# Operand places, the routing's place count and a fourth buffer in a mixture-of-experts block

## The chip, the cores and the metric

One core of one Trainium2 chip runs the whole program. The metric is device time in microseconds (us). The kernel before took 1858.37 us, the median of 3 runs (1856.73 to 1860.6). The engines are TensorE (PE, with its weight loads listed as PEld), VectorE (DVE), ScalarE (ACT), GpSimd (POOL) and SyncE (SP, which issues most of the loads).

## The reference, cut to what matters

One transformer block on 1024 tokens of width 1024: a mixer (an mLSTM half and a dilated-attention half, then `w_out`), and an expert-choice feed-forward layer with 16 experts. All is float32. The part that matters here:

```python
def expert_choice_ffn(h, w_router, b_router, w_gate, w_up, w_down):
    cap = (EC_CAPACITY_FACTOR * S) // N_EXPERTS            # 128 tokens an expert
    affinity = jax.nn.softmax((h @ w_router + b_router), axis=-1)
    gates, idx = lax.top_k(affinity.transpose(0, 2, 1), cap)
    xin = h[bidx, idx]
    hid = jax.nn.silu(xin @ w_gate) * (xin @ w_up)         # 1024 -> 2048, each expert
    y = (hid @ w_down) * gates[..., None]                  # 2048 -> 1024
    return jnp.zeros_like(h).at[bidx, idx].add(y)
```

Each expert's three matrices are 8 MB each in float32, so 384 MB of weights are read once.

## The kernel before, in words

**Split products.** Each float32 product is made of three float32r products: an operand x is split into a high part (ACT copies it to float32r) and a low part (DVE subtracts the high part from x), and xh·wh, xl·wh and xh·wl are summed in PSUM. In a product of 128 by 512 one operand is stationary (its 128 columns are loaded by PEld) and the other moves (512 columns). Each product loads its weights anew.

**Pieces.** A weight matrix of an expert comes in 8 pieces of 128 x 2048 float32 (1 MB). `feed` (L1452) issues the load of the next piece on SP, or on a queue that it is given. `cut` (L1479) takes the oldest loaded piece, makes `wh` on ACT (L1489) and `wl` on DVE (L1490, kept in program order on DVE), and issues the next load into the buffer just freed. `mm` (L1495) runs the 12 products of one piece (L1509) and then calls `cut` once. `wh` and `wl` have CUTS = 3 buffers each, so that the piece being cut during the products of piece n is n + 2. Loaded pieces wait in a ring: RING = 10 buffers (6 of them opened before the router's last steps, EARLY), and 3 more pieces made of borrowed tiles.

**Order of the experts** (`phase_experts`, L1570). For expert e: 8 gate pieces, 8 up pieces, then the 8 down pieces of expert e - 1. Between them stand the transposes of the hidden rows (`expert_hT`, L1538), of the next expert's rows (`expert_xT`, L1525, rows fetched by an indirect load, L1443) and the products that turn a one-hot matrix into row numbers (`route_expert`, L1429). The stationary operands are `xTh` (pool moe1), `xTl` (pool y, tag og) and `hT` (pool ya); the moving ones are `wh` and `wl` (pool moe2).

**Places.** A pool is a stack of tiles on the left or right side of each partition. From the sizes of the pools in their order, `wh`, `wl` and `xTh` begin at a multiple of 512 bytes, `xTl` and `hT` 64 bytes past one. In the projections (L337 to L341, L398 to L400) both operands lie 448 bytes past one. In the output projection (L1174 to L1176) the moving parts lie 192 bytes past one, the stationary ones too, but for three of the four `yal` (64).

**Routing** (`route_sort`, `route_select`). The threshold of each expert is the smallest of its 128 best affinities, found by sorts on DVE in streams that the output projection carries along; the last tile of tokens has its sort in `route_select`. Each sort also keeps the transposed affinities (`keep`, L1308). `route_select` compares them with the threshold (L1398, L1399), counts places by a scan along the row (L1401), adds the counts of the segments before (L1405 to L1411), transposes back (L1414) and makes the first one-hot matrix (L1425).

**What orders the work.** The tile framework's planner orders each engine's queue by its own estimate of when work is ready; an engine then runs its queue strictly in order. `keep_in_program_order` holds an instruction behind the one traced before it on its engine.

Of the kernel before, what the change touches and what calls it, by code (L numbers as in the profile page):

```python
# [11 lines left out]
F32 = mybir.dt.float32  # L12
# [8 lines left out]
P = 128  # L21
# [22 lines left out]

RING = 10
EARLY = 6
FEEDS = (2, 8, 14, 20, 26, 32)
LATE = 3
CUTS = 3
HT = (1, 3, 5, 7)  # L50
# [24 lines left out]
def shape_constants():  # L75

    u = np.arange(F1LEN) - 191
    v1 = np.abs(u) <= 64
    da = np.arange(F2ROW) - 63
    db = np.arange(7) - 3  # L80
    r4 = (4 * da[None, :] + db[:, None]).reshape(-1)
    v4 = np.abs(r4) <= 64
    r16 = np.where(np.abs(da) <= 64, da, 0)
    oh = np.concatenate([_onehot(u, v1), _onehot(4 * r4, v4), _onehot(16 * r16, np.ones(F2ROW, bool))], axis=1)
    mask = np.where(np.concatenate([v1, v4, np.ones(F2ROW, bool)]), 0.0, NEG).astype(np.float32)
    turn = np.concatenate([np.arange(F1LEN)[::-1], F1LEN + np.arange(F2LEN + F2ROW).reshape(-1, F2ROW)[:, ::-1].reshape(-1)])
    oh, mask = oh[:, turn], mask[turn]
    seg, ex = np.divmod(np.arange(P), 32)
    same = ex[:, None] == ex[None, :]
    seg_c = np.stack([same & (seg[:, None] < seg[None, :]), same & (seg[:, None] > seg[None, :])], axis=1).astype(np.float32)  # L90
    return {"c_seg": np.ascontiguousarray(seg_c), "c_oh": np.ascontiguousarray(oh), "c_mask": np.ascontiguousarray(np.broadcast_to(mask, (AH, mask.size)))}

# [17 lines left out]
class K:  # L110
# [3 lines left out]
    def pool(self, name, stack, bufs=1, space=None, side=None):  # L114
# [965 lines left out]
    def route_consts(self, ps):  # L1080
# [7 lines left out]
        self.sort_mem = rt.tile([P, KT, P], F32, name="sort_mem")  # L1088
        self.affT = self.sort_mem[:, 6:8]
        self.r_work, self.bit_a, self.bit_b = (itertools.cycle([self.sort_mem[:, j], self.sort_mem[:, j + 1]]) for j in (0, 2, 4))  # L1090
# [194 lines left out]
    def route_sort(self, i0, n, last=False):  # L1285
# [4 lines left out]
        R = 32 * n  # L1290
        self.copy = nc.vector.tensor_copy if last else lambda o, i: nc.scalar.activation(o, i, AF.Copy)
        mx = rt.tile([P, 4], F32, name="r_mx", bufs=2)[:, :n]
# [13 lines left out]
        nc.tensor.transpose(ps[:R, :P], self.aff[:, i0:i0 + n].rearrange("p s e -> p (s e)"), self.ident)  # L1306

        def keep():  # L1308

            i = i0  # L1310
            while i < i0 + n:
                j = min(i0 + n, i + min((4, 1, 2, 1)[i % 4], (4, 1, 2, 1)[i - i0]))
                self.copy(self.affT[32 * (i % 4):32 * (i % 4 + j - i), i // 4], ps[32 * (i - i0):32 * (j - i0), :P])
                i = j

        w = next(self.r_work).rearrange("p (h t) -> p h t", h=2)
        a, b = next(self.bit_a), next(self.bit_b)
        if n > 2:
# [7 lines left out]
            for r in range(8):  # L1326
                for h in range(2):
                    nc.vector.max(top[h][:, 8 * r:8 * r + 8], src[:, h])
                if r < 7:
                    for h in range(2):  # L1330
                        nc.vector.match_replace(w[:, h], top[h][:, 8 * r:8 * r + 8], src[:, h], -1.0)
                    src = w
                if r == 0:
                    keep()
                yield 0
            nc.vector.tensor_copy(a[:R, 64:], t[:R, ::-1])
        else:
# [3 lines left out]
            for h in range(2):  # L1341
                self.copy(x[h * R:(h + 1) * R], ps[:R, 64 * h:64 * h + 64])
            yield 0
            for r in range(8):
                nc.vector.max(a[R2, 8 * r:8 * r + 8], x)
                if r < 7:
                    nc.vector.match_replace(w, a[R2, 8 * r:8 * r + 8], x, -1.0)
                    x = w
                if r == 0:
                    keep()  # L1350
                yield 0
# [33 lines left out]
    def route_select(self):  # L1385


        nc, rt = self.nc, self.rt
        m = self.yp.tile([P, 8, P], F32, name="sel", tag="og", bufs=MH)
        seg = m[:, 4:6]  # L1390
        nc.scalar.dma_start(out=seg, in_=self.I["c_seg"])
# [4 lines left out]
        for r in range(32, P, 32):  # L1396
            nc.vector.tensor_copy(thr[r:r + 32], thr[:32])
        nc.vector.tensor_scalar(m[:, 0:2], self.affT, thr, None, op0=OP.is_gt)  # L1398
        nc.vector.tensor_scalar(m[:, 2:4], self.affT, thr, None, op0=OP.is_equal)  # L1399
        sc = self.yp.tile([P, 4, P], F32, name="r_scan", tag="og", bufs=MH)  # L1400
        nc.vector.tensor_tensor_scan(sc.rearrange("p j t -> p (j t)"), self.ones[:, 0:1].to_broadcast([P, 4 * P]), m[:, 0:4].rearrange("p j t -> p (j t)"),  # L1401
                                     0.0, OP.mult, OP.add)

        ps = self.psm.tile([P, 512], F32, name="pm")
        nc.tensor.matmul(ps[:, :4], seg[:, 0], sc[:, :, P - 1], start=True, stop=False)  # L1405
        nc.tensor.matmul(ps[:, 1:4], seg[:, 1], sc[:, 0:3, P - 1], start=False, stop=True)
        base = rt.tile([P, 4], F32, name="r_base")
        nc.vector.tensor_copy(base, ps[:, :4])
        for j in range(4):
            nc.vector.scalar_tensor_tensor(sc[:, j], sc[:, j], base[:, j:j + 1], m[:, j], op0=OP.add, op1=OP.mult)  # L1410
        nc.vector.tensor_add(sc[:, 0:2], sc[:, 0:2], sc[:, 2:4])  # L1411
        ps = self.psm.tile([P, 4, P], F32, name="pm")
        for g in range(2):
            nc.tensor.transpose(ps[:, g], sc[:, g], self.ident)  # L1414
        self.route_gates()
        sl = ps[:, 0:2].rearrange("p g (s e) -> p (g s) e", e=32)
        self.onehot(0, sl)
        self.slot = rt.tile([P, NT, 32], F32, name="slot")
        nc.vector.tensor_copy(self.slot, sl)

# [7 lines left out]
    def route_expert(self, e, psum):  # L1428
# [6 lines left out]
        for i in range(NT):  # L1435
            nc.tensor.matmul(ps[:, :5], oh[:, i], self.R[:, i, e], start=(i == 0), stop=(i == NT - 1))
        idx = rt.tile([P, 1], I32, name="idx", bufs=3)
        rg = rt.tile([P, 5], F32, name="rg", bufs=3)
# [5 lines left out]
                                     in_offset=bass.IndirectOffsetOnAxis(ap=idx[:, :1], axis=0))  # L1444
        return dict(idx=idx, gate=rg[:, 0:1], xin=xin)

# [31 lines left out]

    def cut(self):  # L1479

        if not self.fed:
            return
        ts, again = self.fed.pop(0)
        h = self.m2.tile([P, FF], F32R, name="wh", bufs=CUTS)
        l = self.m2.tile([P, FF], F32R, name="wl", bufs=CUTS)
        m = FF // len(ts)
        for j, t in enumerate(ts):
            c = slice(j * m, (j + 1) * m)
            self.nc.scalar.activation(h[:, c], t, AF.Copy)  # L1489
            self.tc.keep_in_program_order(self.nc.vector.tensor_sub(l[:, c], t, h[:, c]))  # L1490
        self.ready.append((h, l))
        if again:
            self.feed(ts)

    def mm(self, xs, n, first, last):  # L1495
# [6 lines left out]
        order = [(q, t, c) for q in range(3) for t in range(FF // N) for c in range(len(ps))]  # L1502
        if last and not (self.fed or self.ready):

# [9 lines left out]

    def expert_xT(self, u, b, psum):

# [7 lines left out]
        for k in range(4 * b, 4 * b + 4):  # L1524
            nc.scalar.activation(f[:, k], ps[:, (k % 4) * P:(k % 4 + 1) * P], AF.Identity, scale=self.a2_col[:, k:k + 1], bias=self.modc[:, KT + k:KT + k + 1])  # L1525
        self.split(h[:, 4 * b:4 * b + 4], l[:, 4 * b:4 * b + 4], f[:, 4 * b:4 * b + 4])
# [38 lines left out]
    def phase_experts(self):  # L1565
# [23 lines left out]
        for b in range(2):  # L1589
            self.expert_xT(u, b, sets[1])  # L1590
        self.ahead = 1
        self.cut()
        p = None
        for e in range(NE):
# [29 lines left out]
def body(tc, I, out):  # L1624
    with ExitStack() as ctx:
# [51 lines left out]
        k.ring = [k.pool("ring_a", st_w, bufs=EARLY)]  # L1677
        k.flow, k.fed, k.ready = k.pieces(), [], []
        k.phase_out()
# [43 lines left out]
```

## Time and profile before

| | us |
|---|---|
| median of 3 runs | 1858.37 |
| the profiled execution | 1857.18 |
| its span | 1855.5 |
| PE busy | 1738.8 |
| DVE busy | 1486.8 |
| ACT busy | 1206.2 |
| first to last expert product (starts, L1509) | 682.8 to 1843 |

Busy time is the sum of an engine's instructions; PE's is modelled and overlaps, so the distance between the starts of two products, and not their length, tells how fast they follow each other. A window is a stretch of the span in us from its start.

### The profile page before, as it was taken

The page shows a single profiled execution, that of the slowest core. Times are in us where ns is not written, and L with a number is a line of the kernel's source. Part 1 is how long each engine was busy: PE and PEld are TensorE (multiplying, and loading weights), DVE is VectorE, ACT ScalarE, POOL GpSimd, SP SyncE. Part 2 cuts the span into 40 slices and gives each one's busy share as a digit, 9 for nine tenths or more (in the row PEclk, how much of TensorE's full clock was granted, in tenths as well). Part 3 has the DMA queues.
Part 4 walks back from the last instruction along what each step waited for, and adds up shares of the span by engine and source line. Part 5 has one row for each costly group of instructions (what it writes and reads, how often), then busy time and mean ns, then how long its engine had stood idle before and what let it go on. Part 6 is the DMA issues. An engine that isn't in the chain of part 4 may idle for free. (4 is left out here: it accounts for less than half of the span.)

```text
span 1855.5 us, 24345 instructions
## 1 busy us (share of the span) xinstructions
PE 1738.8 (94%) x8685; PEld 1400.1 (75%) x8685; DVE 1486.8 (80%) x2147; ACT 1206.2 (65%) x1596; POOL 179.6 (10%) x176
## 2 busy tenths in 40 slices
PE   5999999999998939999999999999999999999997
PEld 4777788778886727888888777787777777777875
DVE  5578885687865778988988888898888888988976
ACT  5346454477763438777777677777776776777764
POOL 1001000031122010011011000100100001000001
PEclk9999999999999959999999999999999999999999
DMA  8135662435648777999999999999999999999991
GB/s 321 47 108 188 208 209 89 108 89 118 139 112 239 270 306 278 382 356 371 392 351 389 348 347 351 362 367 358 352 343 383 349 354 360 336 377 356 357 357 23
DMA packets 150536, 517.39 MB, mean 279 GB/s; under 512 B 32938, under 2 KB 50736, under 8 KB 112784
## 3 DMA queue, kind: packets, MB, share of 16 engines
q1 hardware_dynamic: 136832, 482.07, 70.6%
q0 software_dynamic: 10528, 33.18, 7.1%
q8 instruction: 68, 1.11, 0.2%
q10 hardware_dynamic: 3056, 0.61, 0.2%
q14 instruction: 52, 0.43, 0.1%
HBM read 488.29 MB, written 27.50 MB: 278 GB/s over the span
## 5 line engine op out<-in xcount | busy, mean ns | idle before, releaser
L1490 DVE TENSOR_TENSOR wl<-w,wh 128x2048 fp32r<-128x2048 f32 x295 | 663.2, 2279 | 72.9 <-ACT wh L1489 72.0
L1489 ACT ACTIVATE wh<-w 128x2048 fp32r<-128x2048 f32 x295 | 557.7, 1914 | 120.2 <-PE px L1509 56.3
L1490 DVE TENSOR_TENSOR wl<-w_half,wh 128x1024 fp32r<-128x1024 f32 x178 | 207.9, 1218 | 8.3 <-ACT wh L1489 8.2
L1489 ACT ACTIVATE wh<-w_half 128x1024 fp32r<-128x1024 f32 x178 | 179.8, 1059 | 36.8 <-PE px L1509 16.3
L1509 PE MATMUL px<-wl,xTh 128*128 128x512 f32 x512 | 142.5, 398 | 10.0 <-DVE wl L1490 10.0
L1509 PE MATMUL py<-wl,xTh 128*128 128x512 f32 x512 | 142.6, 398 | 8.9 <-DVE wl L1490 8.8
L1509 PE MATMUL px<-wh,xTh 128*128 128x512 f32 x512 | 141.9, 397 | 3.5 <-ACT wh L1489 1.9
L1509 PE MATMUL py<-wh,xTh 128*128 128x512 f32 x512 | 142.6, 396 | 0.8 <-ACT wh L1489 0.7
L1509 PE MATMUL px<-wh,xTl 128*128 128x512 f32 x512 | 141.4, 397 | 0.0
L1509 PE MATMUL py<-wh,xTl 128*128 128x512 f32 x512 | 141.1, 395 | 0.0
L1509 PE MATMUL px<-wh,hT 128*128 128x512 f32 x512 | 131.5, 397 | 0.0
L1509 PE MATMUL py<-wh,hT 128*128 128x512 f32 x512 | 130.8, 397 | 0.2 <-ACT wh L1489 0.2
L1509 PEld LDWEIGHTS px<-wl,xTh 128*128 128x128 f32 x512 | 94.8, 189 | 38.7 <-DVE wl L1490 18.1
L1509 PEld LDWEIGHTS py<-wl,xTh 128*128 128x128 f32 x512 | 94.1, 188 | 38.1 <-DVE wl L1490 17.8
L1562 POOL DMA_INDIRECT out_dram<-xin,idx x16 | 52.6, 3288 | 661.2 <-DVE xin L1561 661.2
L1509 PEld LDWEIGHTS px<-wh,xTh 128*128 128x128 f32 x512 | 95.2, 189 | 26.6 <-ACT wh L1489 3.6
L1509 PEld LDWEIGHTS px<-wh,xTl 128*128 128x128 f32 x512 | 96.8, 189 | 21.9
L1509 PEld LDWEIGHTS py<-wh,hT 128*128 128x128 f32 x512 | 95.1, 188 | 23.4 <-ACT wh L1489 0.9
L1509 PEld LDWEIGHTS py<-wh,xTh 128*128 128x128 f32 x512 | 94.4, 188 | 24.2 <-ACT wh L1489 3.1
L1509 PEld LDWEIGHTS py<-wh,xTl 128*128 128x128 f32 x512 | 96.1, 188 | 21.8 <-DVE xTl L124 0.2
L1509 PEld LDWEIGHTS px<-wh,hT 128*128 128x128 f32 x512 | 95.0, 188 | 22.6 <-ACT wh L1489 0.4
L398 PE MATMUL pa<-wh,hTh 128*128 128x512 f32 x192 | 78.9, 412 | 1.6 <-ACT wh L355 1.5
(452 smaller groups left out, 3091.9 us busy)
## 6 DMA issues: line engine op xcount, KB each, us to landing
w<-in_w_gate_dram SPq DMA_DIRECT2D x99, 1024.0 KB, 7.3
w<-in_w_down_dram SPq DMA_DIRECT2D x99, 1024.0 KB, 9.6
w<-in_w_up_dram SPq DMA_DIRECT2D x94, 1024.0 KB, 6.2
w_half<-in_w_up_dram SPq DMA_DIRECT2D x62, 512.0 KB, 7.2
w_half<-in_w_gate_dram SPq DMA_DIRECT2D x56, 512.0 KB, 8.2
w_half<-in_w_down_dram SPq DMA_DIRECT2D x56, 512.0 KB, 8.7
ada_w<-in_w_ada_dram SPq DMA_DIRECT2D x64, 256.0 KB, 3.4
wraw<-in_w_in_dram SPq DMA_DIRECT2D x20, 512.0 KB, 4.5
```

Of the source, the lines that this page charges most:

```text
L398: nc.tensor.matmul(ps, hTh[:, k, t], hi[k], start=(k == 0), stop=False)
L1489: self.nc.scalar.activation(h[:, c], t, AF.Copy)
L1490: self.tc.keep_in_program_order(self.nc.vector.tensor_sub(l[:, c], t, h[:, c]))
L1509: nc.tensor.matmul(ps[c], x[:, t], y[:, o:o + 512], start=first and q == 0 and t == 0, stop=last and (q, t) == (2, FF // N - 1))
L1562: nc.gpsimd.indirect_dma_start(out=self.out, out_offset=bass.IndirectOffsetOnAxis(ap=u["idx"][:, :1], axis=0), in_=y, in_offset=None, comp ...
```

## The change: what it does

It adds two unused tiles: 448 bytes ahead of pool `consts` (the first on the left) and 192 bytes ahead of the other tiles of pool `rows` (right). All later tiles of these sides move by as much, so that the expert stage's five operands and those of the output projection all begin at a multiple of 512 bytes. It makes RING 8 and CUTS 4, splits `cut` into a high part (`cut_high`) and the rest, and has ACT make three `wh` during the last sort. It leaves out `keep`, the segments' constant and the scan, and counts the places by 16 bfloat16 products with a triangle and a matrix of ones (built on POOL in `route_consts`). It issues the row fetch of the next expert two pieces later than its one-hot products, and in the first expert lets DVE do every second of the eight scalings in `expert_xT`.

```diff
-RING = 10
+RING = 8
-CUTS = 3
+CUTS = 4
...
+    def fill(self, pool, n):
+        self.nc.gpsimd.memset(pool.tile([P, n // 4], F32, name="fill"), 0.0)
...
     def consts(self):
+        self.fill(cp, 448)
...
-                if r == 0:
-                    keep()
...
             for h in range(2):
-                self.copy(x[h * R:(h + 1) * R], ps[:R, 64 * h:64 * h + 64])
+                if last and h == 0:
+                    nc.vector.tensor_copy(x[h * R:(h + 1) * R], ps[:R, 64 * h:64 * h + 64])
+                else:
+                    nc.scalar.activation(x[h * R:(h + 1) * R], ps[:R, 64 * h:64 * h + 64], AF.Copy)
...
     def route_select(self):
-        for _ in self.route_sort(NT - 1, 1, True):
+        sort = self.route_sort(NT - 1, 1, True)
+        next(sort)
+        next(sort)
+        for _ in range(CUTS - 1):
+            self.cut_high()
+        for _ in sort:
             pass
         thr = rt.tile([P, 1], F32, name="thr")
         nc.vector.tensor_reduce(thr[:32], self.best[:32], axis=AX.X, op=OP.min)
-        # thr to all rows, L1398 to L1414: comparison, scan, segments, transposes
...
+        nc.vector.tensor_copy(row[:32], thr[:32].to_broadcast([32, P]))
+        nc.tensor.transpose(ps[:, :32], row[:32], self.ident[:32, :32])
+        nc.vector.tensor_tensor(m[:, 0], aff, t, OP.is_gt)
+        nc.vector.tensor_tensor(m[:, 1], aff, t, OP.is_equal)
+        nc.tensor.matmul(c, self.upto, m, start=True, stop=False)
+        for i in range(NT):
+            nc.tensor.matmul(c[:, 1], self.all_ones, m[:, 0, i:i + 1, :].to_broadcast([P, NT, NE]), start=False, stop=False)
+        for i in range(1, NT):
+            nc.tensor.matmul(c[:, :, i:], self.all_ones, m[:, :, :NT - i], start=False, stop=(i == NT - 1))
         self.route_gates()
+        nc.vector.tensor_mul(f, c, m)
+        nc.vector.tensor_add(self.slot, f[:, 0], f[:, 1])
+        self.onehot(0, self.slot)
...
-    def cut(self):
+    def cut_high(self):
         if not self.fed:
             return
         ts, again = self.fed.pop(0)
         h = self.m2.tile([P, FF], F32R, name="wh", bufs=CUTS)
+        for j, t in enumerate(ts):
+            act = self.nc.scalar.activation(h[:, j * m:(j + 1) * m], t, AF.Copy)
+            if not self.started:
+                self.tc.keep_in_program_order(act)
+        self.halves.append((ts, h, again))
+
+    def cut(self):
+        if not self.halves:
+            self.cut_high()
+        if not self.halves:
+            return
+        ts, h, again = self.halves.pop(0)
         l = self.m2.tile([P, FF], F32R, name="wl", bufs=CUTS)
...
         if again:
-            self.feed(ts)
+            self.feed(ts, None if self.started else self.nc.gpsimd)
...
             if both and k % 2:
+                nc.vector.tensor_scalar(f[:, k], x, g, z, op0=OP.mult, op1=OP.add)
...
-        u = self.route_expert(0, sets[1])
+        _, u = self.route_expert(0, sets[1])
...
                 if e + 1 < NE and i == 0:
-                    n = self.route_expert(e + 1, X)
+                    route = self.route_expert(e + 1, X)
+                    next(route)
+                if e + 1 < NE and i == 2:
+                    n = next(route)
...
         k.rp = k.pool("rows", st_r, side="right")
+        k.fill(k.rp, 192)
```

## Rows read from the trace of the kernel before

**Rows 1.** The page: PE's busy tenths in 40 slices of the span.

```profile
PE   5999999999998939999999999999999999999997
```

**Rows 2.** Windows: length, then busy time (instructions) by engine, granted clock, DMA share, GB/s.

```profile
core 0: us, PE busy (x) PEld busy (x) DVE busy (x) ACT busy (x) POOL busy (x), PEclk, DMA share, GB/s
...
655.00:665.40 10.40, 0.00 (x0) 0.00 (x0) 9.98 (x71) 0.82 (x1) 0.00 (x0) 0.50 1.00 416
...
812.00:882.00 70.00, 70.00 (x322) 56.93 (x321) 62.02 (x47) 53.99 (x49) 7.49 (x3) 1.00 0.97 374
...
1330.00:1405.00 75.00, 72.21 (x325) 56.91 (x324) 62.39 (x46) 52.49 (x48) 5.91 (x2) 1.00 0.97 360
```

**Rows 3.** Timeline of POOL: start, length; one scatter of rows an expert.

```profile
806.41 5.62 POOL L1562 DMA_INDIRECT out_dram<-xin,idx  x1 [42.29 <-DVE xin L1561]
...
1016.45 3.38 POOL L1562 DMA_INDIRECT out_dram<-xin,idx  x1 [40.81 <-DVE xin L1561]
...
1753.09 1.59 POOL L1562 DMA_INDIRECT out_dram<-xin,idx  x1 [42.07 <-DVE xin L1561]
```

**Rows 4.** Waits from 1040 to 1800 us: total, times, longest.

```profile
DVE wl L1490 <- ACT wh L1489: 65.8, 40, 5.8
...
ACT sort_mem L1525 <- PE py L1523: 22.6, 5, 5.0
...
SPq L1472 <- DVE wl L1490: 427.3, 196, 5.9
```

**Rows 5.** Timeline of all engines from 1044 to 1050 us.

```profile
1046.73 0.17 DVE L1439 COPY rg<-py 128x5 f32<-128x5 f32 x1 [0.79 <-PE py L1436]
...
1049.55 1.20 PE L1509 MATMUL px<-wl,xTh 128*128 128x512 f32 x4 [1.36 <-DVE wl L1490]
```

**Rows 6.** Timeline of PE, products of 512 columns in four stages.

```profile
78.79 0.62 PE L337 MATMUL pa<-hTh,wh 128*128 128x512 f32 x2
...
88.31 0.39 PE L337 MATMUL pb<-hTh,wh 128*128 128x512 f32 x1
...
617.20 0.39 PE L1174 MATMUL pm<-woh,mix 128*128 128x512 f32 x1
...
617.88 0.39 PE L1174 MATMUL pm<-woh,mix 128*128 128x512 f32 x1
...
618.57 0.39 PE L1174 MATMUL pm<-wmh,mix 128*128 128x512 f32 x1
...
714.69 1.09 PE L1509 MATMUL py<-wl,xTh 128*128 128x512 f32 x4
...
725.78 1.09 PE L1509 MATMUL py<-wl,xTh 128*128 128x512 f32 x4
...
1006.23 2.03 PE L1509 MATMUL px<-wh,hT 128*128 128x512 f32 x8
...
1009.03 1.33 PE L1509 MATMUL px<-wh,hT 128*128 128x512 f32 x5
```

**Rows 7.** Timeline of all engines from the last affinities to the first expert product.

```profile
653.62 0.37 PE L1306 MATMUL pm<-ident,aff 128*32 128x128 f32 x1 [7.93 <-DVE aff L1304]
...
655.98 0.28 DVE L1313 COPY sort_mem<-pm 32x128 f32<-32x128 f32 x1
...
665.36 0.27 DVE L1395 TENSOR_REDUCE thr<-sort_mem 32x1 f32<-32x128 f32 x1
...
672.29 1.22 DVE L1425 TENSOR_TENSOR oh<-iota,pm 128x1024 bf16<-128x1024 f32 x1 [0.78 <-PE pm L1414]
...
674.85 4.49 DVE L1490 TENSOR_TENSOR wl<-w,wh 128x2048 fp32r<-128x2048 f32 x2 [0.32 <-issue]
...
682.06 0.65 ACT L123 ACTIVATE xTh<-sort_mem 128x512 fp32r<-128x512 f32 x1
...
682.75 2.08 PE L1509 MATMUL px<-wh,xTh 128*128 128x512 f32 x4 [1.61 <-ACT xTh L123]
684.63 1.91 PE L1509 MATMUL px<-wh,xTl 128*128 128x512 f32 x4
```

More of the change, by code (lines that the diff above doesn't have):

```diff
@@ L87, in shape_constants @@
     oh, mask = oh[:, turn], mask[turn]
[L88 to L91, printed above, removed]
+    return {"c_oh": np.ascontiguousarray(oh), "c_mask": np.ascontiguousarray(np.broadcast_to(mask, (AH, mask.size)))}
 def bc(ap, n, offset=0):
@@ L1088, in route_consts @@
         self.sort_mem = rt.tile([P, KT, P], F32, name="sort_mem")
-        self.affT = self.sort_mem[:, 6:8]
+        tri = self.sort_mem[:, 6]
+        nc.gpsimd.memset(tri, 1.0)
+        self.all_ones = rt.tile([P, P], BF16, name="all_ones")
+        nc.gpsimd.tensor_copy(self.all_ones, tri)
+        nc.gpsimd.affine_select(out=tri, in_=tri, compare_op=OP.is_ge, fill=0.0, base=0, pattern=[[1, P]], channel_multiplier=-1)
+        self.upto = rt.tile([P, P], BF16, name="upto")
+        nc.gpsimd.tensor_copy(self.upto, tri)
         self.r_work, self.bit_a, self.bit_b = (itertools.cycle([self.sort_mem[:, j], self.sort_mem[:, j + 1]]) for j in (0, 2, 4))
@@ L1290, in route_sort @@
         R = 32 * n
-        self.copy = nc.vector.tensor_copy if last else lambda o, i: nc.scalar.activation(o, i, AF.Copy)
         mx = rt.tile([P, 4], F32, name="r_mx", bufs=2)[:, :n]
@@ L1306, in route_sort @@
         nc.tensor.transpose(ps[:R, :P], self.aff[:, i0:i0 + n].rearrange("p s e -> p (s e)"), self.ident)
[L1308 to L1314, printed above, removed]
         w = next(self.r_work).rearrange("p (h t) -> p h t", h=2)
@@ L1348, in route_sort @@
                     x = w
-                if r == 0:
-                    keep()
                 yield 0
@@ L1388, in route_select @@
         nc, rt = self.nc, self.rt
-        m = self.yp.tile([P, 8, P], F32, name="sel", tag="og", bufs=MH)
-        seg = m[:, 4:6]
-        nc.scalar.dma_start(out=seg, in_=self.I["c_seg"])
-        for _ in self.route_sort(NT - 1, 1, True):
+        sort = self.route_sort(NT - 1, 1, True)
[4 more added lines that the diff above has]
+        for _ in sort:
             pass
@@ L1395, in route_select @@
         nc.vector.tensor_reduce(thr[:32], self.best[:32], axis=AX.X, op=OP.min)
[L1396 to L1402, printed above, removed]
@@ L1404, in route_select @@
-        ps = self.psm.tile([P, 512], F32, name="pm")
[L1405 to L1411, printed above, removed]
@@ L1412, in route_select @@
-        ps = self.psm.tile([P, 4, P], F32, name="pm")
-        for g in range(2):
-            nc.tensor.transpose(ps[:, g], sc[:, g], self.ident)
-        self.route_gates()
[L1416 to L1419, printed above, removed]
+        row = self.sort_mem[:, 6]
+        nc.vector.tensor_copy(row[:32], thr[:32].to_broadcast([32, P]))
+        ps = self.psm.tile([P, 512], F32, name="pm")
@@ new lines, in route_select @@
+        nc.tensor.transpose(ps[:, :32], row[:32], self.ident[:32, :32])
+        aff = self.aff[:, :, 0:NE]
+        t = ps[:, 0:NE][:, None, :].to_broadcast([P, NT, NE])
+        m = rt.tile([P, 2, NT, NE], BF16, name="sel")
+        nc.vector.tensor_tensor(m[:, 0], aff, t, OP.is_gt)
+        nc.vector.tensor_tensor(m[:, 1], aff, t, OP.is_equal)
+        ps = self.psm.tile([P, 512], F32, name="pm")
+        c = ps[:, :2 * NT * NE].rearrange("p (g i e) -> p g i e", g=2, i=NT)
+        nc.tensor.matmul(c, self.upto, m, start=True, stop=False)
@@ new lines, in route_select @@
+        for i in range(NT):
+            nc.tensor.matmul(c[:, 1], self.all_ones, m[:, 0, i:i + 1, :].to_broadcast([P, NT, NE]), start=False, stop=False)
+        for i in range(1, NT):
+            nc.tensor.matmul(c[:, :, i:], self.all_ones, m[:, :, :NT - i], start=False, stop=(i == NT - 1))
+        self.route_gates()
+        f = self.sort_mem[:, 6:8].rearrange("p g (i e) -> p g i e", i=NT)
+        nc.vector.tensor_mul(f, c, m)
+        self.slot = rt.tile([P, NT, NE], F32, name="slot")
+        nc.vector.tensor_add(self.slot, f[:, 0], f[:, 1])
@@ L1436, in route_expert @@
             nc.tensor.matmul(ps[:, :5], oh[:, i], self.R[:, i, e], start=(i == 0), stop=(i == NT - 1))
+        yield
         idx = rt.tile([P, 1], I32, name="idx", bufs=3)
@@ L1444, in route_expert @@
                                      in_offset=bass.IndirectOffsetOnAxis(ap=idx[:, :1], axis=0))
-        return dict(idx=idx, gate=rg[:, 0:1], xin=xin)
+        yield dict(idx=idx, gate=rg[:, 0:1], xin=xin)
     def pieces(self):
@@ L1484, in cut @@
         h = self.m2.tile([P, FF], F32R, name="wh", bufs=CUTS)
+        m = FF // len(ts)
+        for j, t in enumerate(ts):
[9 more added lines that the diff above has]
+        ts, h, again = self.halves.pop(0)
         l = self.m2.tile([P, FF], F32R, name="wl", bufs=CUTS)
@@ L1488, in cut @@
             c = slice(j * m, (j + 1) * m)
-            self.nc.scalar.activation(h[:, c], t, AF.Copy)
             self.tc.keep_in_program_order(self.nc.vector.tensor_sub(l[:, c], t, h[:, c]))
@@ L1502, in mm @@
         order = [(q, t, c) for q in range(3) for t in range(FF // N) for c in range(len(ps))]
-        if last and not (self.fed or self.ready):
+        if last and not (self.fed or self.halves or self.ready):
             order.sort(key=lambda a: (a[1], a[0], a[2]))
@@ L1513, in mm, with expert_xT @@
             self.cut()
-    def expert_xT(self, u, b, psum):
+    def expert_xT(self, u, b, psum, both=False):
         nc = self.nc
@@ L1524, in expert_xT @@
         for k in range(4 * b, 4 * b + 4):
-            nc.scalar.activation(f[:, k], ps[:, (k % 4) * P:(k % 4 + 1) * P], AF.Identity, scale=self.a2_col[:, k:k + 1], bias=self.modc[:, KT + k:KT + k + 1])
+            x, g, z = ps[:, (k % 4) * P:(k % 4 + 1) * P], self.a2_col[:, k:k + 1], self.modc[:, KT + k:KT + k + 1]
+            if both and k % 2:
+                nc.vector.tensor_scalar(f[:, k], x, g, z, op0=OP.mult, op1=OP.add)
+            else:
+                nc.scalar.activation(f[:, k], x, AF.Identity, scale=g, bias=z)
         self.split(h[:, 4 * b:4 * b + 4], l[:, 4 * b:4 * b + 4], f[:, 4 * b:4 * b + 4])
@@ L1589, in phase_experts @@
         for b in range(2):
-            self.expert_xT(u, b, sets[1])
+            self.expert_xT(u, b, sets[1], True)
+        self.started = True
         self.ahead = 1
@@ L1677, in body @@
         k.ring = [k.pool("ring_a", st_w, bufs=EARLY)]
-        k.flow, k.fed, k.ready = k.pieces(), [], []
+        k.flow, k.fed, k.halves, k.ready, k.started = k.pieces(), [], [], [], False
         k.phase_out()
```

## The prediction

> **What bounds the kernel now.** I read the page first, then windows of the expert stage, then who waits there, then single products. The page shows PE near full in all slices but a few [rows 1]: the reader is to see that the only hole of size is slice 15, from 649 to 696 us (a slice is 1855.5 / 40 = 46.4 us), the routing. A busy share of nine tenths doesn't say that PE can go no faster, so the next question is how fast the experts follow each other. One scatter of rows is issued an expert [rows 3]. From 806.41 to 1016.45 are three experts, 70.0 us each; from 1016.45 to 1753.09 are ten, 73.66 us each. The work of every expert is the same (24 pieces of 12 products), so each late expert loses 3.66 us that an early one doesn't: 36.6 us in ten.
>
> The waits of the late stretch say where [rows 4]: PE's weight loads and products wait for `wl` from DVE, DVE for `wh` from ACT, ACT for PE. No row has ACT waiting for a load; the loads wait for DVE to free a buffer (427.3 us in 196 waits), so memory isn't the bound. The engines aren't full either: in 70 us DVE is busy 62.02 and ACT 53.99, in a late 75 us 62.39 and 52.49 [rows 2]. It is a matter of order and of too few finished pieces: at 1046.73 DVE stands 0.79 us for the one-hot products of the next expert, subtractions queue behind it, and at 1049.55 PE waits 1.36 us for `wl` [rows 5]. PE is the bound in early experts, the chain ACT to DVE to PE in late ones.
>
> The last question is the distance of the products themselves [rows 6]. In gate and up pieces four pieces take 725.78 - 714.69 = 11.09 us, 231.0 ns a product. In a down piece 12 products take 1009.03 - 1006.23 = 2.80 us, 233.3 ns. In the projection, whose operands all lie 448 bytes past a multiple of 512, 42 products take 88.31 - 78.79 = 9.52 us, 226.7 ns. In the output projection three products with both operands at 192 take 0.68 us (617.20 to 617.88), the next three, of which one has its stationary operand at 64, take 0.69 us (to 618.57). Equal places go with some 227 ns, unequal ones with 230 to 233.
>
> **The change part by part.**
>
> *The two fills.* There are 16 x 24 x 12 = 4608 expert products. 128 of the 384 pieces are down pieces, now wholly unequal (hT at 64, `wh` and `wl` at 0); of a gate or up piece a third is unequal (`xTl` at 64). After the fills all are at 0. At best all take 226.7 ns: 256 pieces x 12 x 4.3 ns = 13.2 us, and 128 x 12 x 6.6 ns = 10.1 us, in all 23 us. At worst the cause of the slower distance is another (the engines and loads that write SBUF beside it, which the projection has less of): 0. I take 228 ns, since the projection is the nearest row with everything equal but has fewer loads beside it: 256 x 12 x 3.0 + 128 x 12 x 5.3 = 9.2 + 8.1 = **17 us** less. All of it lies on PE, which sets the end of the stage. In the output projection 0.01 us in three products is nothing.
>
> The Trainium skill, page TensorE: Matmul & The Clock Gate, section Part 2: What happens when you issue a matmul, says that PE has two independent SBUF read ports, so that loading the next weights takes no read bandwidth from the running product. By it the place of an operand would be without effect, and the first term 0. The rows speak against it weakly, 226.7 against 231.0 and 233.3; it is the second rival's case.
>
> *The fourth buffer.* With CUTS 4 the piece cut behind piece n is n + 3, so one more finished piece of 2.77 us (11.09 / 4) stands before PE when DVE or ACT is late. The waits for `wl` are shorter than that (1.36 us in the row shown), and so covered one by one. The longest kind of cause isn't: ACT stands up to 5.0 us in its queue for the transposes of the next expert's rows [rows 4]. The row fetch moved two pieces later takes DVE's 0.79 us wait away: the products are long done at i = 2. What the move costs: the indirect load is issued some 5.5 us later, and has six pieces (three up, three down, 17 us) left until its transposes, so it is late for nobody; POOL has only the scatter beside it, issued a stage earlier. What is late next is DVE itself, 62.0 us of work in an expert that then takes 70.0 - 1.1 = 68.9 us. Bounds: 0 (the order in ACT's queue keeps the stalls) to 36.6 us (every late expert runs as an early one). I take 0.8 us a late expert as left, a third of the 2.2 us by which a wait of 5.0 exceeds the cover (it stands in some experts only), hence 36.6 - 8 = **29 us** less.
>
> *RING 8.* 11 pieces instead of 13 circulate, 11 x 2.75 = 30 us from a buffer's release to its use in place of 36. A load must be issued, land and wait within that. An issue finds its queue ready at once, since SP waits for buffers alone; I price it at 0, and if that cover is gone it is the fourth rival.
>
> *Routing.* From the threshold's reduction to the first one-hot matrix are now 672.29 - 665.36 = 6.93 us [rows 7]. After: the reduction 0.27; the row copy, two comparisons, a product with the counts and an addition, at 0.28 each by the copy of 32x128, 1.4; a transpose, 0.37; hand-overs between DVE and PE, two, say 0.2 together; and 16 products. Their columns are 256 + 8 x 128 + 2 x 16 x (7 + ... + 1) = 2176. Four products of 512 columns take 684.63 - 682.75 = 1.88 us just after, 0.92 ns a column, so 2.0 us. Sum 4.2, gain 2.7 us. Bounds: 231.0 ns for 512 columns makes 1.0 us, gain 3.7; each of the 16 as dear as 512 columns (0.47) makes 7.5, a loss of 2.8. Leaving out `keep` saves its 0.28 us copy on DVE, which is busy 9.98 of 10.40 us there [rows 2]. Making three `wh` on ACT during the sort is hidden (ACT is busy 0.82 us in that stretch), but three `wl` then stand on DVE ahead of its half of the scalings: 3 x 2.25 = 6.7 us from 674.85 to 681.6 on the time scale of now, after which two scalings (0.28 each by the copy) and ACT's `xTh` (0.65) lead to 682.8 where 682.75 stands now: 0, with bounds of 0.9 either way (the three subtractions ahead of the scalings, or a third behind them). The POOL feeds stand behind the first row fetch, with nothing of the path behind them. Routing: **3 us** less, bounds -5 to +4.
>
> *POOL's new constants* (a memset, copies, a select of 128x128) go beside the output projection; by the copy's 0.28 us at most 2 us in POOL's queue, at 0.
>
> **Sum.** 1857.18 (the profiled execution, span 1855.5) - 17 - 29 - 3 = 1808. The median of 3 runs is 1.2 us higher, which I leave within the range.
>
> **The rivals.**
>
> 1. *The stalls stay.* ACT's queue is ordered by the planner's estimate, and where a scaling or an activation that waits for PE stands ahead of `wh`, a buffer more doesn't help. For it: waits of up to 5.0 us, against 2.77 of cover; the early experts had none with three buffers, so order and not depth made them. Against: `wl` waits seen are half a piece. Time: 1857.2 - 17 - 3 = 1837.
> 2. *The fills do nothing*, the distance is of the stage and not of the place. For it: fewer loads run beside the projection. Against: within the output projection the distance changes from one triple to the next. Time: 1857.2 - 29 - 3 = 1825. Together with the first: 1854.
> 3. *Slower: the loads become the bound.* Place: the ring of 11 pieces. For it: the DMA share is 0.97 at 374 GB/s and also at 360 [rows 2], as if full at both. If 360 GB/s were what 16 engines can sustain, an expert of 70 us x 374 = 26.2 MB would take 72.7 us. It decides once the two pieces less of ring no longer carry a stretch that wants more than 360: then all 16 experts take 72.7, 2.7 more for the early five and 1 less for the late ten, and the late ones add the wait behind the load, which I price at one issue gap of 2.77 us each for ten: 1857.2 + 13.5 - 10 + 27.7 - 3 = 1885 at most, 1872 with half of those gaps. Against: 416 GB/s for 10 us [rows 2].
>
> The Trainium skill, page DMA: Bandwidth & Descriptors, section Specifications, gives about 358 GB/s as the limit from HBM for a core. By that rule the third rival holds. The trace disagrees: 374 GB/s over 70 us and 416 over 10 [rows 2].
>
> **How the numbers follow.** The forecast, 1808, has 0.54, its own range 1797 to 1820 (spacing 11 to 23, stalls 24 to 36, routing 1 to 4). Rival 1 (1837) has 0.17, rival 2 (1825) 0.12, both together (1854) 0.06, rival 3 (1872) 0.06, and 0.05 lies below 1797, where all bounds are met at once (1857.2 - 23 - 36.6 - 5 = 1793). The range 1794 to 1842 holds the forecast and the first two rivals and leaves out some 0.17. What can be told from no change is 0.2%, 3.7 us. Slower is rival 3, 0.06; within 0.2% half of the case of both, 0.03; faster the rest, 0.91.
>
> **What would show it.** The distance of products: a down piece at 2.74 us or under and a gate piece at 2.73 show the fills right, 2.80 and 2.77 show them empty. The scatters of the late experts 69 us apart show the fourth buffer right; over 72 shows rival 1, and then rows of PE waiting for `wl` with ACT's `sort_mem` ahead. A row of ACT's `wh` waiting for a load shows rival 3. Threshold to one-hot in 4 us shows the products' price. The forecast is wrong if the first product doesn't start before 682 or a late expert takes more than 71 us.

## The result, and the profile after

The changed kernel takes 1835.92 us (median of 4 runs, 1833.95 to 1838.39), the kernel before 1857.57 beside it: a ratio of 0.9879, 95% interval 0.9864 to 0.9893. That is 21.7 us less where 49 were forecast; it lies in the range, but it is the time of the first rival (1837) and not of the forecast (1808). The profiled execution took 1833.95 us, its span 1832.0; it is the fastest of the four.

The page of the changed kernel, PE's busy tenths in 40 slices, for [rows 1]:

```profile
PE   5999999989998939999999999999999999999997
```

As before it shows PE nearly full, and says no more. The places of the experts do; POOL's timeline, one scatter an expert, for [rows 3]:

```profile
801.71 5.62 POOL L1581 DMA_INDIRECT out_dram<-xin,idx  x1 [37.05 <-DVE xin L1580]
...
1007.20 1.58 POOL L1581 DMA_INDIRECT out_dram<-xin,idx  x1 [33.27 <-DVE xin L1580]
...
1736.15 1.59 POOL L1581 DMA_INDIRECT out_dram<-xin,idx  x1 [44.07 <-DVE xin L1580]
```

Three early experts take (1007.20 - 801.71) / 3 = 68.5 us each, the next ten (1736.15 - 1007.20) / 10 = 72.9. Before they took 70.0 and 73.66. Closer products alone give 18.4 / 16 = 1.15 us an expert (the 18.4 is worked out below), and a late one gained 0.8: the 3.66 us by which a late expert was longer are all still there, now 4.4. Over 72 us was the sign named for the first rival.

Its windows, for [rows 2] (length; busy time and instructions of PE, its weight loads, DVE, ACT, POOL; granted clock, DMA share, GB/s):

```profile
811.00:880.00 69.00, 69.00 (x322) 57.01 (x322) 62.78 (x47) 54.21 (x49) 8.24 (x2) 1.00 0.98 385
1330.00:1405.00 75.00, 73.30 (x337) 59.71 (x336) 66.01 (x53) 55.47 (x51) 5.57 (x3) 1.00 0.97 373
```

PE is busy throughout an early expert, and loses 1.70 us of 75 in the late stretch even by this coarse count.

The waits of the changed kernel from 1040 to 1800 us (total, times, longest), for [rows 4]:

```profile
DVE wl L1505 <- ACT wh L1489: 67.5, 40, 5.5
ACT sort_mem L1544 <- PE py L1538: 39.2, 5, 10.7
ACT sort_mem L1544 <- PE px L1538: 34.7, 7, 7.6
ACT hid L1622 <- PE px L1524: 32.5, 5, 7.1
ACT hid L1622 <- PE py L1524: 28.6, 5, 6.5
...
ACT wh L1489 <- PE px L1524: 9.9, 14, 1.1
ACT wh L1489 <- PE py L1524: 8.8, 15, 0.8
...
PE py L1538 <- DMA xin<-h_d,idx: 3.7, 2, 2.2
...
ACT wh L1489 <- DMA w_half<-in_w_down_dram: 0.8, 1, 0.8
```

and of the kernel before, in the same stretch:

```profile
ACT wh L1489 <- PE px L1509: 36.7, 41, 1.6
ACT wh L1489 <- PE py L1509: 29.4, 34, 1.1
...
ACT sort_mem L1525 <- PE px L1523: 19.3, 7, 5.3
```

The reader is to see three things. DVE's wait for `wh` is as it was (67.5, before 65.8). ACT waited 66.1 us for PE to give a buffer back and now waits 18.7; it stands in its queue instead, behind scalings (`sort_mem`) and silus (`hid`) that wait for PE, 135.0 us in these four rows and 77.8 before, and its longest stand for the transposes has grown from 5.3 to 10.7 us. And it waits for two single loads only, 0.8 us each.

PE's products in the changed kernel, a gate stretch and two down pieces, for [rows 6]:

```profile
690.36 1.07 PE L1524 MATMUL px<-wh,xTl 128*128 128x512 f32 x4
...
701.24 1.07 PE L1524 MATMUL px<-wh,xTl 128*128 128x512 f32 x4
...
980.01 1.98 PE L1524 MATMUL px<-wh,hT 128*128 128x512 f32 x8
...
982.73 1.98 PE L1524 MATMUL px<-wh,hT 128*128 128x512 f32 x8
```

Four pieces take 10.88 us (before 11.09), 226.7 ns a product; a down piece 2.72 us (before 2.80). Both meet the bounds named (2.73 and 2.74). The 4607 distances between the stage's products add up to 1160.3 us before and 1139.9 after. Those of up to 260 ns average 231.96 ns before and 227.96 after; all 4607 at these averages make 1068.6 and 1050.2 us, 18.4 less. The rest is what I call PE's stalls: 91.7 us before, 89.7 after.

The timeline of all engines from the last affinities to the first product, for [rows 7]:

```profile
649.07 0.37 PE L1314 MATMUL pm<-ident,aff 128*32 128x128 f32 x1 [5.89 <-DVE aff L1312]
...
661.68 0.27 DVE L1397 TENSOR_REDUCE thr<-sort_mem 32x1 f32<-32x128 f32 x1
...
666.14 1.22 DVE L1426 TENSOR_TENSOR oh<-iota,slot 128x1024 bf16<-128x1024 f32 x1
...
668.43 6.70 DVE L1505 TENSOR_TENSOR wl<-w,wh 128x2048 fp32r<-128x2048 f32 x3
668.48 3.17 POOL L1445 DMA_INDIRECT xin<-h_d,idx  x1 [4.98 <-DVE rg L1443]
...
675.34 1.97 PE L1538 MATMUL py<-ident,xin 128*128 128x128 f32 x8 [7.54 <-DMA xin<-h_d,idx]
...
679.36 2.07 PE L1524 MATMUL px<-wh,xTh 128*128 128x512 f32 x4 [2.05 <-ACT xTh L124]
```

Threshold to one-hot takes 666.14 - 661.68 = 4.46 us (before 6.93, forecast 4.2). But one-hot to first product takes 13.22 us where it took 10.46, and 2.1 of these 2.8 us more are POOL's issue of the row fetch, which lasted 3.17 us instead of 1.05 beside three subtractions on DVE. The first product still starts 3.4 us earlier, because the threshold stands 3.7 us earlier, and that lies ahead of the routing: the last affinities are transposed at 649.07 us, before at 653.62.

### The profile page after: what moved, and what is told of

Read it like the earlier page. It is cut to its first block, busy times and chain, and to the rows that moved or that the text cites. A ratio compares the mean times of both kernels' runs of the same rounds, so it can differ in the third digit from the quotient of the medians.

```text
span 1832.0 us, 24429 instructions
## 1 busy us (share of the span) xinstructions
PE 1722.9 (94%) x8696; PEld 1402.8 (77%) x8696; DVE 1487.1 (81%) x2156; ACT 1197.7 (65%) x1603; POOL 180.5 (10%) x185
## 5 line engine op out<-in xcount | busy, mean ns | idle before, releaser
L1505 DVE TENSOR_TENSOR wl<-w,wh 128x2048 fp32r<-128x2048 f32 x278 | 627.8, 2285 | 81.6 <-ACT wh L1489 81.2
L1489 ACT ACTIVATE wh<-w 128x2048 fp32r<-128x2048 f32 x278 | 523.1, 1919 | 55.2 <-PE py L1524 26.3
L1505 DVE TENSOR_TENSOR wl<-w_half,wh 128x1024 fp32r<-128x1024 f32 x210 | 245.6, 1217 | 8.6 <-ACT wh L1489 8.5
L1489 ACT ACTIVATE wh<-w_half 128x1024 fp32r<-128x1024 f32 x210 | 211.8, 1058 | 24.1 <-PE px L1524 13.1
L1524 PEld LDWEIGHTS py<-wh,xTl 128*128 128x128 f32 x512 | 96.0, 188 | 20.4 <-DVE xTl L125 0.2
L1581 POOL DMA_INDIRECT out_dram<-xin,idx x16 | 48.3, 3019 | 590.6 <-DVE xin L1580 590.6
L1445 POOL DMA_INDIRECT xin<-h_d,idx x16 | 37.8, 2362 | 477.9 <-DVE rg L1443 197.4
```

Source lines behind the costliest of these rows:

```text
L1445: nc.gpsimd.indirect_dma_start(out=xin, out_offset=None, in_=self.h2_d, in_offset=bass.IndirectOffsetOnAxis(ap=idx[:, :1], axis=0))
L1489: act = self.nc.scalar.activation(h[:, j * m:(j + 1) * m], t, AF.Copy)
L1524: nc.tensor.matmul(ps[c], x[:, t], y[:, o:o + 512], start=first and q == 0 and t == 0, stop=last and (q, t) == (2, FF // N - 1))
L1581: nc.gpsimd.indirect_dma_start(out=self.out, out_offset=bass.IndirectOffsetOnAxis(ap=u["idx"][:, :1], axis=0), in_=y, in_offset=None, comp ...
```

## The experiments

The theory after the first reading: ACT's order makes the stalls, so that a buffer may be free and ACT still stand. Rivals: DVE is too full (62.78 us busy in 69); the loads bound the late experts. All ratios are to the kernel before, run beside each.

**e1, `wh` alone held in written order.**

```
-            if not self.started:
-                self.tc.keep_in_program_order(act)
+            self.tc.keep_in_program_order(act)
```

> The changed kernel with one edit: every activation that makes a wh is held behind what is traced before it on ACT, in all experts and not only ahead of the first. Theory (order): the late experts lose time because ACT's queue, as the planner orders it, has activations that wait for PE (the gate's silu, the scaling of the next rows, hT) ahead of a wh that could already be made; at 1027.40 of the changed kernel ACT had stood 5.91 us for py. With wh in traced order the late experts run as the early ones, 69 us each instead of 71.8: 10 x 2.8 = 28 us less, about 1808. Rival (DVE is too full): 62.6 us of DVE work in a 69 us expert can't be kept fed, whatever ACT's order: within 5 us of 1836. Rival (loads): the same, within 5 us of 1836, and a wh waiting for a load in the rows.

Measured 1839.58 us, ratio 0.9893 (0.9875 to 0.9911): no gain, a miss. From expert 5 on ACT's order was the same instruction for instruction. The hold ties a `wh` to the instruction written before it; it doesn't keep silu, scalings and `hT`, which aren't held, from getting ahead of it. So the run tried half of the theory; e5 tries the whole.

**e2, three buffers and ten ring tiles, the rest of the change kept.**

```
-RING = 8
+RING = 10
...
-CUTS = 4
+CUTS = 3
```

> The changed kernel with CUTS 3 and RING 10 (two wh made during the sort instead of three): the fourth buffer alone undone. If the fourth buffer did nothing because ACT's order keeps the stalls, late experts take the same 71 to 72.5 us and the time is 1833 to 1841. If it took part of the stalls away, late experts go back toward 73.66 - 1.1 = 72.6 us, and to over 73 if it carried more than the forecast gave it: 1841 to 1850. If the two loaded pieces less cost something, it is below 1833.

Measured 1830.28 us, 0.9852 (0.9835 to 0.9868): the fourth buffer with the shorter ring isn't worth 29 us, it costs 5.6 if anything (the intervals overlap a little). A time below 1833 was named as the sign that the two ring tiles less cost something; the run undoes both at once and can't tell. The waits for loads (two of 0.8 us in the changed kernel) speak against the ring. The waits of e2 from 1040 to 1800 us:

```profile
ACT wh L1489 <- PE px L1524: 35.8, 45, 1.3
ACT wh L1489 <- PE py L1524: 32.3, 41, 1.1
...
ACT sort_mem L1544 <- PE py L1538: 22.0, 5, 4.9
ACT hid L1622 <- PE px L1524: 19.2, 5, 4.3
ACT sort_mem L1544 <- PE px L1538: 18.8, 7, 5.2
...
ACT hid L1622 <- PE py L1524: 15.6, 5, 4.3
```

The scalings and silus stand 75.6 us here and 135.0 with four buffers, and `wh` waits for PE 68.1 here and 18.7 there. The reading: the fourth buffer let ACT run a piece ahead, into instructions that wait for PE, as often as before (22 times in these rows) and longer.

**e3, the change without the fills; e4, the kernel before with the fills alone.**

```
-        self.fill(cp, 448)
...
-        k.fill(k.rp, 192)
```

> The changed kernel without its two fills: xTl and hT lie 64 bytes past a multiple of 512 again. If place sets the distance, gate and up pieces go back to 2.77 us and down pieces to 2.80, 231 and 233 ns a product where they are 227 now, and the time rises by 17 us to 1853 (less if the late experts are held by ACT and not by PE: 10 experts would then lose nothing, and the rise is 6 to 10 us). If the distance fell for another reason, pieces stay at 2.72 and the time at 1836.

> The kernel before with the two fills alone. If place sets the distance: pieces of 2.72 us, early experts 69 us, and 1857.6 - 17 = 1841, or up to 1851 if the late experts are held by ACT's order and take 73.66 us as before. If place does nothing: 1857.

e3 measured 1852.76 us, 0.9968 (0.995 to 0.9986): the fills are worth 16.8 us to the changed kernel, as forecast. e4 measured 1845.11, 0.9925 (0.9909 to 0.9942), 12.6 us less than before; its products stand 227 ns apart, but PE's stalls are 96.0 us (before 91.7), and its first product starts at 685.19, 2.4 us later than before.

**e5, every activation of the expert stage held; e6, DVE's work too; e7, e5 with e2's sizes.** `pin` holds an instruction in written order once the experts have started.

```
+    def pin(self, ins):
+        if self.started:
+            self.tc.keep_in_program_order(ins)
...
-        self.nc.scalar.activation(hi, src, AF.Copy)
+        self.pin(self.nc.scalar.activation(hi, src, AF.Copy))
...
-                nc.scalar.activation(f[:, k], x, AF.Identity, scale=g, bias=z)
+                self.pin(nc.scalar.activation(f[:, k], x, AF.Identity, scale=g, bias=z))
...
```

> The changed kernel, with every activation of the expert stage (wh, silu, the scalings of xT, the high parts of xT and hT) held in the order in which the program writes them, so that none that waits for TensorE can stand ahead of a wh whose buffer is free by more than the program says. Theory, the order of ACT's queue makes the stalls: experts 5 to 14 fall from 71.9 to about 69 us each, the early ones' 68.9, and the whole is 1835.9 - 10 x 2.9 = about 1808 us (1800 to 1815). Rival, VectorE is too full (62.7 busy of some 69 us) and the order is only where it shows: 1830 to 1842. Rival, the loads bound the late experts: 1830 to 1842, and wh is seen to wait for DMAs as soon as ACT is in order.

> As the kernel before it, and VectorE's low parts of xT and hT, its products with silu and its last multiplication of y held in written order too. Theory, order on ACT alone: the same as e5 within 5 us. If VectorE's order makes stalls of its own, this one is faster than e5 by more than 5 us. Rival, VectorE too full or the loads: 1830 to 1842.

> e5 with three buffers of pieces and ten tiles in the ring, as before the change. Theory, order: once ACT is in order the fourth buffer is not needed or is worth at most some us, 1805 to 1818. If the fourth buffer does its work only when the order lets it, this one is slower than e5 by 10 to 30 us. Rivals (VectorE, loads): 1827 to 1840, as 1830 without the order.

e5 measured 1808.52 us, 0.9738 (0.9709 to 0.9767); e6 1798.26, 0.9682 (0.9652 to 0.9711); e7 1800.79, 0.9698 (0.9668 to 0.9728); e7's median is 7.7 us below e5's, but from the first expert product to the last they take 1108.0 and 1109.4. The late experts of e6, POOL's timeline:

```profile
1009.83 3.37 POOL L1586 DMA_INDIRECT out_dram<-xin,idx  x1 [32.63 <-DVE xin L1585]
...
1696.14 5.59 POOL L1586 DMA_INDIRECT out_dram<-xin,idx  x1 [34.55 <-DVE xin L1585]
```

Ten experts at 68.63 us: late ones now run as early ones, with every load and every instruction of the changed kernel in place. How that comes about shows at the end of an expert's gate. The changed kernel, timeline of all engines (an entry in brackets is the idle time before, and who ended it):

```profile
1019.57 1.91 ACT L1489 ACTIVATE wh<-w 128x2048 fp32r<-128x2048 f32 x1
...
1022.44 1.07 PE L1524 MATMUL py<-wh,xTh 128*128 128x512 f32 x4
...
1025.16 1.07 PE L1524 MATMUL py<-wh,xTh 128*128 128x512 f32 x4
...
1027.40 1.57 ACT L1622 ACTIVATE hid<-py 128x512 f32<-128x512 f32 x3 [5.91 <-PE py L1524]
...
1028.84 1.93 ACT L1489 ACTIVATE wh<-w 128x2048 fp32r<-128x2048 f32 x1
...
1030.80 2.29 DVE L1505 TENSOR_TENSOR wl<-w,wh 128x2048 fp32r<-128x2048 f32 x1 [3.81 <-ACT wh L1489]
```

ACT is done at 1021.48 and stands 5.91 us for the last product of the gate, with silu at its head. PE began new pieces at 1022.44 and 1025.16, so it had given two buffers back; nobody cut into them, and DVE then stood 3.81 us for a `wh`. The same place in e6, ACT's timeline:

```profile
1020.86 1.92 ACT L1495 ACTIVATE wh<-w 128x2048 fp32r<-128x2048 f32 x1 [1.71 <-PE py L1529]
...
1026.30 2.01 ACT L1495 ACTIVATE wh<-w_half 128x1024 fp32r<-128x1024 f32 x2 [0.80 <-PE py L1529]
...
1029.25 2.07 ACT L1627 ACTIVATE hid<-py 128x512 f32<-128x512 f32 x4 [0.46 <-PE py L1529]
```

Each buffer is cut as PE gives it back, and silu waits 0.46 us. Both rivals fall: the loads are the same, and DVE, with the same work, is simply busier, as e6's window shows:

```profile
1330.00:1405.00 75.00, 75.00 (x352) 62.25 (x351) 69.66 (x53) 57.15 (x55) 8.11 (x2) 1.00 0.98 391
```

PE has no idle time left in it. PE's stalls in e6 are 53.3 us where the changed kernel had 89.7. DVE's own order is worth another 10.3 us (e5 to e6, whose intervals just touch): with ACT alone held, DVE still stood for PE in e5 with `hid` 15.4 + 13.6 us and with the output's `xin` 20.4 + 13.6 us from 1040 to 1800.

**e8, half of the reloads left out.**

```
+        self.turn = not self.turn
+        if self.started and self.turn:
+            self.fed.append((ts, not once))
+            return
```

> The changed kernel with every second reload of a weight piece left out once the experts have started (the old piece is used again, so the weights are wrong): half the bytes, the same work on every engine. ACT's order is planned anew with them. Theory, the planner puts work that waits for TensorE ahead of wh because it counts the loads as late: late experts 69 us, about 1808. Rival, real loads: the same or better, 1795 to 1810, so this run separates the two only with e5 (where the loads stay). Rival, VectorE too full: no gain, 1830 to 1840.

Measured 1800.83 us, 0.9689 (0.966 to 0.9718). Where a load is left out the old piece is used again. Nothing is held here, yet ACT's order came out without the stands, and ten late experts took 68.7 us each. It fits an order that is made from an estimate with late loads, but real loads are fewer here too; that the stands go with all the real loads in place is shown by e5 and e6.

**e9, e6 with three buffers and ten ring tiles.** The edits of e6 and e2 together.

> The changed kernel with ACT and VectorE held in written order in the expert stage (e6, 1798.3), and with three buffers of pieces and ten ring tiles as before the change. Theory, the fourth buffer buys nothing once the order is held and costs at the start, since a third subtraction wl is already queued when the rows of expert 0 are fetched (GpSimd's issue took 3.17 us with four buffers, 1.05 with three): 1798.3 - 2.1 = about 1796, and down to 1790 if e7's whole 7.7 us over e5 come again. Rival, the fourth buffer does its work once the order lets it: slower than e6, 1803 to 1815.

Measured 1795.57 us, 0.9669 (0.9656 to 0.9683), the fastest of all. Against e6 (0.9682, 0.9652 to 0.9711) it can't be told apart: from the first expert product to the last it takes 1100.9 us and e6 1100.8. With the order right too, the fourth buffer with the shorter ring brings nothing. The row fetch of expert 0 in e2's timeline, with two subtractions at hand instead of three:

```profile
671.04 1.05 POOL L1445 DMA_INDIRECT xin<-h_d,idx  x1 [4.98 <-DVE rg L1443]
671.28 4.49 DVE L1505 TENSOR_TENSOR wl<-w,wh 128x2048 fp32r<-128x2048 f32 x2 [0.34 <-issue]
```

**e11, the kernel before, with the order held and nothing else.** The holds of e6 put into the kernel before.

> The kernel before the change with nothing but the order of ACT and VectorE held in the expert stage as in e6: three buffers in one part, no fills, the old routing. Theory: the late experts fall from 73.6 us to the early ones' 70.0, 1857.7 - 10 x 3.6 = about 1822 (1817 to 1828), so the order is worth more than the whole change. Rival, the buffer in two parts is needed for it: 1840 to 1858.

Measured 1837.19 us, 0.9896 (0.988 to 0.9913): 19.4 us, not 36. A miss. Its late experts take 71.1 us, its early ones 70.6. An up piece of expert 6, timeline of all engines:

```profile
1120.47 0.17 DVE L1445 COPY rg<-px 128x5 f32<-128x5 f32 x1 [1.65 <-PE px L1442]
...
1120.95 4.49 DVE L1496 TENSOR_TENSOR wl<-w,wh 128x2048 fp32r<-128x2048 f32 x2
...
1123.29 1.19 PE L1515 MATMUL py<-wl,xTh 128*128 128x512 f32 x4 [1.35 <-DVE wl L1496]
```

This is the pair of [rows 5], larger: DVE stands for the one-hot products, and PE then for `wl`. The groups by line of DVE's copies of `rg` from 1040 to 1740 us, e11:

```profile
L1445 DVE COPY rg<-py 128x5 f32<-128x5 f32 x5 | 0.8, 166 | 11.2 <-PE py L1442 11.2
L1445 DVE COPY rg<-px 128x5 f32<-128x5 f32 x5 | 0.8, 165 | 11.0 <-PE px L1442 11.0
```

and e9:

```profile
L1447 DVE COPY rg<-px 128x5 f32<-128x5 f32 x5 | 0.8, 158 | 0.0
L1447 DVE COPY rg<-py 128x5 f32<-128x5 f32 x4 | 0.7, 163 | 2.7 <-PE py L1443 2.7
```

22.2 us of DVE's stands became 2.7: in e9 the row numbers of the next expert are taken two pieces after their products, and the held order alone doesn't remove these stands. On PE, closer products (1068.2 to 1047.0 us, as above), fewer stalls (69.7 to 53.9) and the start (first product at 680.64 instead of 682.56) make 38.9 us, about the difference of the two profiled spans (1833.0 and 1794.4); the medians lie 41.6 apart. How much of the 15.8 us of stalls is the later copy of the row numbers and how much the cut in two parts isn't shown.

**e10 and e12, other offsets.** The fill of the constants at 192 and at 320 bytes; `xTl` and `hT` then stand 256 or 128 bytes from `wh` and `wl`.

```
-        self.fill(cp, 448)
+        self.fill(cp, 192)
```

> The changed kernel with the fill of the constants at 192 bytes instead of 448: xTl and hT then stand 256 bytes away from wh and wl modulo 512, xTh stays equal. Theory, the offset counts modulo 512 as the change says: products with xTh stay at 227 ns, those with xTl go to about 231 and those with hT to about 233, which is (1024 x 4 + 1536 x 6) ns = some 13 us more, 1849. Rival, it counts modulo 256 or less: all stay at 227 ns, 1836.

> As e10, with the fill of the constants at 320 bytes: xTl and hT stand 384 bytes past a multiple of 512, wh, wl and xTh at 0. e10 kept 227 ns at a difference of 256, so the offset doesn't count modulo 512. Theory, it counts modulo 256: products with xTl and hT go to 231 and 233 ns, down pieces to 2.80 us, about 1849. Rival, it counts modulo 128 or less: all stay at 227 ns, down pieces at 2.72 us, about 1837.

Down pieces of e10, PE's timeline:

```profile
986.92 1.98 PE L1524 MATMUL px<-wh,hT 128*128 128x512 f32 x8
...
989.64 1.98 PE L1524 MATMUL px<-wh,hT 128*128 128x512 f32 x8
```

and of e12:

```profile
987.74 2.03 PE L1524 MATMUL px<-wh,hT 128*128 128x512 f32 x8
...
990.53 2.02 PE L1524 MATMUL px<-wh,hT 128*128 128x512 f32 x8
```

2.72 us at a difference of 256, 2.79 at 128. One run each took 1839.36 and 1849.56 us, beside 1856.58 and 1857.92 before. A difference of 256 is as good as none, so the offset doesn't count modulo 512; as far as the differences tried go (0, 64, 128, 256), it counts modulo 256.

## Why the prediction was wrong

*Fills: right.* 17 forecast from 228 ns a product; 227.96 ns and 18.4 us by the trace, 16.8 by e3, 12.6 by e4. That the equal offset and not the stage makes 227 ns is shown by e12, where the same stage goes back to 2.79 us. The second rival is out. The Trainium skill, TensorE: Matmul & The Clock Gate, Part 2: What happens when you issue a matmul, has the loading of the next weights take nothing from the running product, through two independent read ports; for these operands a product costs 4 to 6 ns more when their places differ, and by which way isn't shown.

*Fourth buffer: the step that failed*, 29 us forecast; PE's stalls fell by 2.0 (91.7 to 89.7). The prediction said that waits for `wl` of 1.36 us are "covered one by one" by one more piece of 2.77, and that of ACT's longest stand of 5.0 us (5.3 in the row shown above) only the excess of 2.2 is left. Both compare a wait with a depth, as if ACT's stand were of a fixed length and began whatever the depth. It ends when PE reaches a given product, and it begins when ACT has done what is queued ahead of it; a buffer more lets ACT arrive earlier and stand longer (75.6 us in e2, 135.0 with four buffers). That the stands are what costs the late experts is shown by e5 and e6: with the order held, the same loads and the same work, a late expert takes 69.3 and 68.63 us. The first rival said so, and its evidence (early experts ran at 70.0 with three buffers) was in the prediction's own rows: where experts of equal depth differ, depth need not be what the slower ones lack. I gave it 0.17 because the waits on PE were short, but the wait to weigh was ACT's, ahead of a free buffer.

*The row fetch, two pieces later*, stood in the same term as a wait of 0.79 us. DVE's stands at `rg` from 1040 to 1800 us fell from 11.8 to 1.2. e4 to e2, that is the buffer in two parts, this move and the routing, without the fourth buffer, are 14.8 us, and PE's stalls go from 96.0 to 83.4; no run takes these parts one by one. "Late for nobody" was nearly right: twice the transposes stood for the rows, 3.7 us together.

*RING 8: priced at 0, rightly as far as the loads go.* The third rival (the term on the ring calls it the fourth) is out: ACT waits for loads twice, 0.8 us each, e6 moves 391 GB/s from 1330 to 1405 us, and with the order held, eight ring tiles with four buffers and ten with three take the same (e6, e9). The limit of some 358 GB/s (the Trainium skill, DMA: Bandwidth & Descriptors, Specifications) is exceeded in this stretch. Whether the shorter ring changes the planner's order isn't shown.

*Routing: it looks right by luck.* The chain gained 2.5 us, near the 2.7 worked out. The three subtractions, priced at 0, took 2.8 us back, 2.3 of them from POOL's issue to the landed rows (6.86 against 4.54). And from the last affinities to the threshold it is 12.6 us where it was 11.7. From the last affinities to the first product it is 29.0 to 29.2 us in the three kernels with the old routing, 29.9 to 30.3 in the eight with the new one and four buffers, and 27.9 to 28.0 in the three with the new one and three buffers: the routing is worth some 1 us by itself, and with the fourth buffer it costs 1. The 3.4 us that show lie ahead of it, in last affinities that stand 4.6 us earlier (649.07 against 653.62). In e10, whose instructions on ACT and PE have the same order as the changed kernel's throughout, they stand at 655.17 and the first product at 685.18. So the order alone doesn't make this spread, and the profiled execution of the changed kernel was an early one.

The sum in medians: fills -12.6 (e4), two parts, later row fetch and routing -14.8 (e2), fourth buffer and shorter ring +5.6.

*Open:* why the order turns bad at expert 5. e8 points to the estimate of the loads, without separating it from the loads themselves. Nor is it shown how much of e5 to e6 is `hid` and how much the output, nor what four buffers do with a ring of ten, or three with a ring of eight.

## What to carry to other kernels

Before adding a buffer, look at both waits of the engine that fills it: for a free buffer, and in its queue for something else. Here the kernel before had 66.1 us of the one and 77.8 of the other; with a fourth buffer and a shorter ring the first fell to 18.7, the second grew to 135.0, and PE gained 2.0. Where the next thing in the queue waits for the engine that is to be fed, the order must be changed. Where equal work takes longer late than early, the early part shows what the order can reach: holding it was worth 37.7 us to the changed kernel, more than the whole change. A hold must cover all that competes in the queue: holding `wh` alone did nothing.

## What the hardware showed that was not expected

Products of 512 columns stand 227 ns apart when both operands lie at the same offset or 256 bytes apart (so, as far as tried, at the same offset modulo 256), and some 232 to 233 when they differ by 64 or 128 (2.72 against 2.79 to 2.80 us for 12). POOL's issue of the first expert's row fetch took 1.05 us in the six kernels with two subtractions on DVE behind the routing and 3.17 us in the eight with three: in the changed kernel a subtraction began 0.05 us ahead of the issue, in e2 0.24 behind it. The first subtraction ends at 668.43 + 6.70 / 3 = 670.66, and 1.05 us later, at 671.71, would be the end of an issue that waited for it; it ended at 671.65. That POOL waited is so far an argument from times. The Trainium skill, SBUF — State Buffer, section SBUF: two separate sides, describes such a lock: VectorE and GpSimd share a pair of ports, and of a VectorE instruction with two inputs in SBUF and a GpSimd one that reads SBUF, whichever starts first holds the pair to its end while the other is blocked. The times agree with it, 0.05 us ahead in the one case and 0.24 behind in the other; that the issue, whose row numbers lie in SBUF, is such a reading instruction isn't shown by any run.
